# Rows of token operands at 258 words instead of 256, and weight halves at one of eight 8-byte offsets, in a float32 two-model kernel on one core

## The chip, the cores and the metric

The kernel runs on one core of a Trainium2 chip. The metric is the device time of one execution in microseconds; lower is better. A figure of "before" is the median of three runs unless the text names the profiled execution.

## The reference

A sequence of 256 tokens of width 1024 goes through two small models, all in float32. The first is a gated mixer followed by a feed-forward layer:

```python
h = rmsnorm(x, norm_mix_g); proj = h @ w_in
u, v, bg, cg, xs, ga, gb = split(proj)
a = gelu(u) * (chunk-masked mix of rmsnorm(gelu(v)) over 128 tokens)
c = bg * causal_dwconv(cg * xs)
x = x + (sigmoid(ga) * (a @ w_proj_a) + sigmoid(gb) * (c @ w_proj_b)) @ w_out
z = relu(rmsnorm(x) @ w_ff1); x = x + (z * z) @ w_ff2
```

The second has two layers. The first layer's mixer is differential attention with 8 heads, the second's is latent attention with 16 heads; each is followed by a convolutional feed-forward layer (up to 5632 columns, three-tap causal convolution, silu gate, down to 1024). A final RMS norm gives the output. Nearly all the arithmetic is in the products of 256 tokens with weight matrices.

## The kernel before, in words

Activations are kept transposed: a tile `[128, 8, 256]` holds 1024 features as 8 rows `k` of 128 features, each row 256 tokens long. These tiles come from `b8` (line 110), a ring of seven buffers. Smaller ones with four rows come from `b4` (line 113, five buffers), pairs of rows from `t2` (line 116, ten buffers).

For accuracy every float32 product is made of three fast matmuls. An operand `w` is split into `hi`, its rounded half, and `lo`, the remainder, and `mm3` (line 195) adds `hi*xh`, `hi*xl` and `lo*xh` into one PSUM bank; every matmul of these products is issued from line 193. The moving operand is normally a row of tokens (256 columns) and the stationary one a 128x128 block of a weight half. In `token_group` (line 395) and `last_rows` (line 937) the roles are swapped: 128 tokens are stationary and 512 columns of a weight half move.

Weights stream from HBM in pieces of 1024 columns (512 KB). `run` (line 142) goes through a list of steps in program order; ahead of each it loads raw pieces (line 165, on SP's queue, up to five ahead) and splits units (`split_to`, line 168): ScalarE writes `hi` (line 178), VectorE subtracts to get `lo` (line 179). Both halves have a ring of seven buffers, and splitting runs three units ahead of use, so a `hi` buffer comes free when TensorE has finished with the unit that held it.

`group` (line 207) computes four column blocks for eight rows `k`: one row with four column blocks is 12 matmuls, and one unit serves two rows. `rows` (line 222) takes one unit per row and makes all eight column blocks of it, 24 matmuls. So in a `group` the row changes every 12 matmuls and the unit every 24; in `rows` both change every 24.

A row of a `b8` tile begins 1024 bytes after the one before it, a row of a `b4` tile too; a buffer of a weight half is 4096 bytes, and a 128-column block begins 512 bytes after the one before it. Seen modulo 512 bytes, then, the start of the moving row and the start of the weight block stand in one fixed relation all through the kernel, whichever buffers, rows and blocks are at work.

The tiles named `v` (lines 430, 703, 1000) and the final `xt` (line 926) use buffers of the same ring as `b8`, in the shapes `[128, 2, 1024]` and `[128, 2048]`.

Of the kernel before, what the change touches and what calls it, by code (L numbers as in the profile page):

```python
# [11 lines left out]
F32R = mybir.dt.float32r  # L12
# [4 lines left out]
P = 128  # L17
T = 256
D = 1024
# [6 lines left out]
DA_SCALE = 64 ** -0.5  # L26
MLA_SCALE = 96 ** -0.5
LAMBDA_INIT = 0.8 - 0.6 * float(np.exp(-0.3 * 0))
WARM = 11
NEG = float(np.finfo(np.float32).min)  # L30

# [53 lines left out]
class Builder:  # L85
# [22 lines left out]
        return self.act.tile(shape, dt, tag=tag, bufs=bufs, name=self.name(tag))  # L108

    def b8(self, dt=F32):  # L110
        return self.t([P, 8, T], "b8", 7, dt)

    def b4(self, shape, dt=F32):
        return self.t([P] + shape, "b4", 5, dt)
# [27 lines left out]
    def run(self):  # L142
        order, seen = [], set()
        for units, _ in self.steps:
            for u in units:
                if id(u) not in seen:
                    seen.add(id(u))
                    order.append(u)
        at = {id(u): i for i, u in enumerate(order)}
        raws, rat = [], {}  # L150
        for u in order:
            if id(u.raw) not in rat:
                rat[id(u.raw)] = len(raws)
                raws.append(u.raw)
        done = {"split": 0, "raw": 0}

        def load_to(i):
            while done["raw"] <= min(i, len(raws) - 1):
                r = raws[done["raw"]]
                r.tile = self.rawp.tile([P, 1024], F32, tag="raw", name=self.name("raw"))  # L160
                n = r.size if done["raw"] else r.size // 2
                for j, o in enumerate(range(0, r.size, n)):
                    for dst, src in self.before.get((done["raw"], j), ()):
                        self.nc.sync.dma_start(out=dst, in_=src)
                    self.nc.sync.dma_start(out=r.tile[:, o:o + n], in_=r.src[:, o:o + n])
                done["raw"] += 1

        def split_to(i):
            while done["split"] <= min(i, len(order) - 1):
                u = order[done["split"]]  # L170
                load_to(rat[id(u.raw)] + self.RAW_AHEAD)
                w = u.raw.tile[:, u.off:u.off + u.size]
                hi = self.unitp.tile([P, 1024], F32R, tag="hi", name=self.name("hi"))
                lo = self.unitp.tile([P, 1024], F32R, tag="lo", name=self.name("lo"))
                n = u.size if done["split"] else u.size // 2
                for o in range(0, u.size, n):
                    sl = slice(o, o + n)
                    self.last_hi = self.nc.scalar.copy(hi[:, sl], w[:, sl])  # L178
                    (u.eng or self.nc.vector).tensor_tensor(  # L179
                        lo[:, sl], w[:, sl], hi[:, sl].bitcast(F32), op=ALU.subtract)  # L180
                u.hi, u.lo = hi[:, :u.size], lo[:, :u.size]
                done["split"] += 1

        load_to(2)
        split_to(1)
        for units, fn in self.steps:
            if units:
                split_to(max(at[id(u)] for u in units) + self.AHEAD)
            fn()
# [158 lines left out]
    def setup(self):  # L348
# [9 lines left out]
        ps = self.at_bank()  # L358
        for _ in range(WARM):
            nc.tensor.matmul(ps[:, 0, 0:P], self.ones, self.ones, start=True, stop=True)  # L360
# [54 lines left out]
    def mixer(self):  # L415
# [7 lines left out]
        bufs = {}  # L423
# [3 lines left out]

        def v_evac(h):
            if h == 0:
                bufs["v"] = self.t([P, 2, D], "b8", 7)  # L430
                bufs["ssv"] = self.t([P, 2, 2], "ssv", 1)
            v = bufs["v"]
            for b in range(2):
                o = v[:, b, h * 512:(h + 1) * 512]
                nc.scalar.activation(o, vb[h][b].rearrange("p a t -> p (a t)"), AF.Gelu,
                                     scale=st["rt"][:, b:b + 1])
                sq = self.t2()
                nc.scalar.activation(sq.rearrange("p a t -> p (a t)"), o, AF.Square,
                                     accum_out=bufs["ssv"][:, h, b:b + 1])
# [13 lines left out]
        def S(pr):  # L453
            def fn():
                with self.tc.issue_after(self.last_hi.ins):
# [4 lines left out]
                         between={0: (N(1),), 2: (N(2),), 4: (N(3), S(0)), 6: (S(1),), 7: (S(2),)})  # L460
        self.token_group(g[1], vb[1], KD, xh, xl,
                         between={0: (S(3),), 2: (one,), 5: (two, lambda: v_evac(0))})
        self.step(lambda: v_evac(1))
        self.step(v_norm)

# [179 lines left out]
    def diff_attention(self):  # L645
# [4 lines left out]
        st, bufs = {}, {}  # L650

        def one():
# [24 lines left out]
            nc.vector.tensor_tensor(nl, e[:, 1:2], e[:, 0:1], op=ALU.subtract)  # L677
            nc.vector.tensor_scalar(nl, nl, -LAMBDA_INIT, None, op0=ALU.add)
            st["nl"] = nl
            gs = self.const.tile([P, 1], F32, name="g_sub")  # L680
            nc.vector.tensor_scalar(gs, self.par("g_sub"), 1.0 - LAMBDA_INIT, None, op0=ALU.mult)
            st["gs"] = gs
# [17 lines left out]

        def v_evac(h):
            if h == 0:
                bufs["v"] = self.t([P, 2, D], "b8", 7)
                bufs["oh"], bufs["ol"] = self.b8(F32R), self.b8(F32R)
            for b in range(2):
                nc.scalar.activation(bufs["v"][:, b, h * 512:(h + 1) * 512],
                                     vb[h][b].rearrange("p a t -> p (a t)"), AF.Copy,
                                     scale=st["rt"][:, b:b + 1])
# [107 lines left out]
        for p in range(4):  # L816
            bt = {}
            if p == 0:
                bt[2] = (two, lambda: v_evac(0))
                bt[6] = (normed,)  # L820
            if p >= 1:
                bt[4] = (L(scores, 2 * p - 2),)
                bt[5] = (L(scores, 2 * p - 1),)
            if p >= 2:
                bt[3] = (L(trans, p - 2),)
                bt[6] = (L(values, p - 2),)
                bt[7] = (L(out_t, p - 2),)
            bk = []
            self.group(wqk[4 * p:4 * p + 4], bk, 4, xh, xl, between=bt)
            self.step(lambda p=p, bk=bk: qk_evac(p, bk))  # L830
        self.token_group(wv[4:], vb[1], KD, xh, xl,
                         between={0: (L(trans, 2),), 2: (L(scores, 6),), 4: (L(scores, 7),)})
        self.step(lambda: v_evac(1))
        wo = self.weights(a["da_w_o"], 2048, 2)
        oh, ol = lambda k: bufs["oh"][:, k, :], lambda k: bufs["ol"][:, k, :]
# [86 lines left out]
    def turn_x(self, b, c):  # L922

        nc = self.nc
        if b == 0 and c == 0:
            self.xt = self.b8().rearrange("p k t -> p (k t)")
            self.g_last = self.b4([D])
            nc.sync.dma_start(out=self.g_last, in_=self.a["g_last"])
            self.last_sq = self.t([P, 2, 2], "lsq", 1)
        ps = self.at_bank().rearrange("p a t -> p (a t)")  # L930
        for i in range(4):
            nc.tensor.transpose(ps[:, i * P:(i + 1) * P],
                                self.x[:, 4 * c + i, b * P:(b + 1) * P], self.ident)
        o = b * D + c * 512
        nc.scalar.copy(self.xt[:, o:o + 512], ps)
# [46 lines left out]
    def mla(self):  # L982
# [7 lines left out]
        st, skv, sq_, bufs = {}, {}, {}, {}  # L990
# [5 lines left out]
        def tables():  # L996
            ml = self.b4([2, 2, T])
            nc.sync.dma_start(out=ml, in_=a["ml_tab"])
            self.ml_c, self.ml_s = ml[:, 0], ml[:, 1]
            bufs["v"] = self.t([P, 2, D], "b8", 7)  # L1000
            bufs["ke"], bufs["ko"] = self.b8(), self.b8()
            bufs["oh"], bufs["ol"] = self.b8(F32R), self.b8(F32R)
            nc.gpsimd.memset(bufs["ke"][96:128, :, :], 0.0)
            nc.gpsimd.memset(bufs["ko"][0:32, :, :], 0.0)
# [78 lines left out]
        def k_evac(h):  # L1083
            for i in range(2):
                sl = slice(4 * h + 2 * i, 4 * h + 2 * i + 2)
                for key, o in (("ke", 0), ("ko", 64)):
                    nc.scalar.copy(bufs[key][o:o + 64, sl, :], kb[h][i][o:o + 64])

        self.step(tables)
        self.group(w_ckv, kvb, 3, xh, xl)  # L1090
        self.step(one)
# [225 lines left out]
```

## Time and profile before

| | before |
|---|---|
| median of three runs (lowest to highest) | 1029.93 us (1027.82 to 1030.82) |
| the profiled execution, its own time | 1023.16 us |
| its span, first to last instruction | 1021.4 us |
| TensorE busy | 997.7 us (98%) |
| VectorE, ScalarE, GpSimd busy | 745.1, 569.7, 175.0 us |
| HBM read over the span | 178.04 MB, 175 GB/s |
| mean granted TensorE clock | 0.994 of full speed |

The profiled execution is 6.8 us shorter than the median of the runs, and 1.8 us of its time lie outside the span. A matmul's busy time counts its whole passage through the array, and consecutive matmuls overlap; a matmul of 256 columns is listed at 280 ns though a new one starts every 113 to 118 ns. The number to look at is therefore the pitch, the time from one start to the next, which the chain of waits gives: a piece of the chain divided by the matmuls in it.

### The profile page before, as it was taken

What the parts mean: (1) busy time and instruction counts of PE and PEld (TensorE: products, weight loads), DVE (VectorE), ACT (ScalarE), POOL (GpSimd) and SP (SyncE); (2) the same over time, 40 slices, a digit from 0 to 9 for tenths busy, and PEclk for the clock granted to TensorE, in tenths of its full rate; (3) what the DMA queues carried; (4) which work ended last, traced back from release to release, by engine and by line L of the source; (5) the groups of instructions that cost most, each with busy time, mean ns of one, the idle gap of its engine ahead of it and who ended that gap; (6) DMA issues with size and microseconds to landing.
All of it is one profiled execution on the core that took longest, in us unless ns stands there. A gap on an engine that the chain in (4) does not pass through costs nothing.

```text
span 1021.4 us, 19659 instructions
## 1 busy us (share of the span) xinstructions
PE 997.7 (98%) x7940; PEld 960.3 (94%) x7940; DVE 745.1 (73%) x1124; ACT 569.7 (56%) x895; POOL 175.0 (17%) x121
## 2 busy tenths in 40 slices
PE   8999999999999999989899999999998999999996
PEld 7999999999999999978799999999987899999995
DVE  5667766567656665778868887777889988887774
ACT  6644454445444444846576665555686667655553
POOL 2101300002311221452102201010422121100001
PEclk9999999999999999999999999999999999999999
DMA  9675555554555555353345465555553435655531
GB/s 334 220 259 170 185 184 185 189 187 159 202 196 190 194 194 195 113 206 129 109 159 187 158 209 181 194 181 160 176 168 127 145 114 195 205 190 185 187 104 41
DMA packets 51067, 180.36 MB, mean 177 GB/s; under 512 B 5664, under 2 KB 6176, under 8 KB 50976
## 3 DMA queue, kind: packets, MB, share of 16 engines
q1 hardware_dynamic: 50688, 178.58, 51.9%
q8 instruction: 62, 1.02, 0.4%
q10 hardware_dynamic: 288, 0.52, 0.1%
q14 instruction: 29, 0.24, 0.1%
HBM read 178.04 MB, written 1.05 MB: 175 GB/s over the span
## 4 chain that ended last, share of the span: by engine, by line
PE 88%; DVE 3%; ACT 3%; issue 2%; POOL 2%; DMA 1%; SPq 0%; POOLq 0%; DVEq 0%; ACTq 0%
PE mm L193 60%; PE at L193 24%; DVE lo L179 1%; ACT hi L178 1%; POOL tiny L308 1%; POOL xg L697 1%; DMA raw<-in_w_in 1%; PE at L1119 1%; DVE t L870 1%; PE at L1142 1%; ACT b L741 0%; ACT t L1129 0%; POOL t L869 0%; PE at L489 0%; PE at L1118 0%
## 5 line engine op out<-in xcount | busy, mean ns | idle before, releaser
L193 PE MATMUL mm<-b,hi 128*128 128x256 f32 x3584 | 638.6, 280 | 1.1 <-DVE b L1031 0.8
L193 PEld LDWEIGHTS mm<-b,hi 128*128 128x128 f32 x3584 | 547.9, 188 | 5.1 <-issue 2.1
L179 DVE TENSOR_TENSOR lo<-raw,hi 128x1024 fp32r<-128x1024 f32 (+2 forms) x336 | 416.6, 1251 | 181.9 <-ACT hi L178 180.9
L178 ACT CAST hi<-raw 128x1024 fp32r<-128x1024 f32 (+2 forms) x337 | 345.4, 1037 | 301.5 <-PE mm L193 230.4
L193 PE MATMUL mm<-b,lo 128*128 128x256 f32 x1792 | 499.9, 279 | 0.0
L193 PEld LDWEIGHTS mm<-b,lo 128*128 128x128 f32 x1792 | 336.7, 188 | 0.7 <-issue 0.7
L193 PE MATMUL at<-b,hi 128*128 128x256 f32 x1088 | 190.9, 278 | 1.0 <-POOL b L337 1.0
L193 PEld LDWEIGHTS at<-b,hi 128*128 128x128 f32 x1088 | 165.0, 188 | 2.2 <-POOL b L337 1.2
L193 PE MATMUL at<-b,lo 128*128 128x256 f32 x544 | 151.0, 278 | 0.0
L193 PEld LDWEIGHTS at<-b,lo 128*128 128x128 f32 x544 | 102.0, 187 | 0.0
L894 POOL TENSOR_TENSOR t<-t,t 128x512 f32<-128x512 f32 x22 | 40.3, 1833 | 289.9 <-DVE t L597 251.4
L597 DVE SCALAR_TENSOR_TENSOR t<-t,par,t 128x254 f32<-128x254 f32 (+1 forms) x176 | 76.0, 485 | 11.6 <-ACT t L595 11.0
L280 POOL TENSOR_TENSOR t<-t,t 128x512 f32<-128x512 f32 x18 | 26.0, 1445 | 197.5 <-ACT t L279 196.9
L193 PE MATMUL at<-hi,b 128*128 128x512 f32 x176 | 56.7, 394 | 0.0
L336 ACT CAST b<-t 128x512 fp32r<-128x512 f32 x50 | 30.9, 621 | 43.1 <-POOL t L894 36.4
L331 DVE TENSOR_TENSOR t<-mm,rbc 128x512 f32<-128x512 f32 x76 | 51.6, 687 | 0.2
L337 POOL TENSOR_TENSOR b<-t,b 128x512 fp32r<-128x512 f32 x16 | 29.7, 1864 | 119.6 <-ACT b L336 119.6
L193 PE MATMUL mm<-hi,b 128*128 128x512 f32 x144 | 48.8, 411 | 1.1 <-ACT hi L178 1.1
L595 ACT ACTIVATE t<-t,par 128x256 f32<-128x256 f32 x88 | 46.0, 591 | 6.4 <-DVE t L331 6.4
L337 DVE TENSOR_TENSOR b<-t,b 128x512 fp32r<-128x512 f32 x34 | 24.2, 718 | 23.0 <-ACT b L336 23.0
L193 PEld LDWEIGHTS at<-hi,b 128*128 128x128 f32 x176 | 32.9, 187 | 7.7
L193 PEld LDWEIGHTS mm<-hi,b 128*128 128x128 f32 x144 | 27.8, 194 | 8.2 <-ACT hi L178 1.9
(181 smaller groups left out, 709.2 us busy)
## 6 DMA issues: line engine op xcount, KB each, us to landing
raw<-in_ffn_up SPq DMA_DIRECT2D x88, 512.0 KB, 4.8
raw<-in_w_ff SPq DMA_DIRECT2D x64, 512.0 KB, 4.5
raw<-in_w_in SPq DMA_DIRECT2D x55, 512.0 KB, 4.8
raw<-in_ffn_down SPq DMA_DIRECT2D x44, 512.0 KB, 4.1
raw<-in_da_qk SPq DMA_DIRECT2D x16, 512.0 KB, 4.8
raw<-in_w_proj_a SPq DMA_DIRECT2D x8, 512.0 KB, 4.1
raw<-in_w_proj_b SPq DMA_DIRECT2D x8, 512.0 KB, 3.7
raw<-in_w_out SPq DMA_DIRECT2D x8, 512.0 KB, 4.9
```

The source lines that it names most:

```text
L178: self.last_hi = self.nc.scalar.copy(hi[:, sl], w[:, sl])
L179: (u.eng or self.nc.vector).tensor_tensor(lo[:, sl], w[:, sl], hi[:, sl].bitcast(F32), op=ALU.subtract)
L193: self.nc.tensor.matmul(out, lhsT, rhs, start=start, stop=stop, skip_group_check=True)
L280: nc.gpsimd.tensor_tensor(self.ss, self.ss, sq, op=ALU.add)
L308: self.nc.gpsimd.tensor_tensor(r, ms, self.mhalf[:, :n], op=ALU.pow)
L331: self.nc.vector.tensor_tensor(o, bank, self.over2(r), op=ALU.mult)
L336: self.nc.scalar.copy(hi, src)
L337: (eng or self.nc.vector).tensor_tensor(lo, src, hi.bitcast(F32), op=ALU.subtract)
L595: nc.scalar.activation(y, z, AF.Identity, scale=w[2], bias=bias)
L597: nc.vector.scalar_tensor_tensor(out=y[:, d:], in0=z[:, :T - d], scalar=w[2 - d], in1=y[:, d:], op0=ALU.mult, op1=ALU.add)
L697: nc.gpsimd.tensor_tensor(xp, xp, self.over2(st["rx"]), op=ALU.mult)
L894: nc.gpsimd.tensor_tensor(y[0], y[0], y[1], op=ALU.mult)
```

## The change

A `b8` tile gets rows of 258 words and its users see a view of the first 256 of each row; a row then begins 1032 bytes after the one before it. The `v` and `xt` tiles are made as large as the new buffer, with `v`'s two rows 1032 words apart and `xt` contiguous. The buffers of both weight halves grow from 1024 to 1040 words, and the unit with number n in the order of splitting lies at word 2n mod 16 of its buffers, so at one of eight offsets of 0 to 56 bytes; `hi` and `lo` of a unit have the same one. No instruction is added or removed and the order is the same. `b4` and `t2` tiles and the residual `x` stay as they were.

```diff
+XPAD = 2
+WPAD = 16
...
     def b8(self, dt=F32):
-        return self.t([P, 8, T], "b8", 7, dt)
+        t = self.t([P, 8, T + XPAD], "b8", 7, dt)
+        return t[:, :, :T]
...
-                hi = self.unitp.tile([P, 1024], F32R, tag="hi", name=self.name("hi"))
-                lo = self.unitp.tile([P, 1024], F32R, tag="lo", name=self.name("lo"))
+                hi = self.unitp.tile([P, 1024 + WPAD], F32R, tag="hi", name=self.name("hi"))
+                lo = self.unitp.tile([P, 1024 + WPAD], F32R, tag="lo", name=self.name("lo"))
+                o = 2 * done["split"] % WPAD
+                hi, lo = hi[:, o:o + 1024], lo[:, o:o + 1024]
...
-                bufs["v"] = self.t([P, 2, D], "b8", 7)
+                bufs["v"] = self.t([P, 2, D + 4 * XPAD], "b8", 7)[:, :, :D]
...
-            self.xt = self.b8().rearrange("p k t -> p (k t)")
+            self.xt = self.t([P, 8 * (T + XPAD)], "b8", 7)[:, :8 * T]
```

The line of `v` is changed in the same way in three places.

## Rows read from the trace of the kernel before

**Rows 1.** The page, part 1: busy time, share and instructions of each engine.

```profile
PE 997.7 (98%) x7940; PEld 960.3 (94%) x7940; DVE 745.1 (73%) x1124; ACT 569.7 (56%) x895; POOL 175.0 (17%) x121
```

**Rows 2.** The page, part 4: the chain that ended last, by line.

```profile
PE mm L193 60%; PE at L193 24%; DVE lo L179 1%; ACT hi L178 1%; POOL tiny L308 1%; POOL xg L697 1%; DMA raw<-in_w_in 1%; PE at L1119 1%; DVE t L870 1%; PE at L1142 1%; ACT b L741 0%; ACT t L1129 0%; POOL t L869 0%; PE at L489 0%; PE at L1118 0%
```

**Rows 3.** Groups by line and form, PE: xcount | busy us, mean ns | idle.

```profile
L193 PE MATMUL mm<-b,hi 128*128 128x256 f32 x3584 | 638.6, 280 | 1.1 <-DVE b L1031 0.8 <-ACT b L706 0.2
L193 PE MATMUL mm<-b,lo 128*128 128x256 f32 x1792 | 499.9, 279 | 0.0
L193 PE MATMUL at<-b,hi 128*128 128x256 f32 x1088 | 190.9, 278 | 1.0 <-POOL b L337 1.0
L193 PE MATMUL at<-b,lo 128*128 128x256 f32 x544 | 151.0, 278 | 0.0
L193 PE MATMUL at<-hi,b 128*128 128x512 f32 x176 | 56.7, 394 | 0.0
L193 PE MATMUL mm<-hi,b 128*128 128x512 f32 x144 | 48.8, 411 | 1.1 <-ACT hi L178 1.1
L193 PE MATMUL at<-lo,b 128*128 128x512 f32 x88 | 34.7, 394 | 0.0
L193 PE MATMUL mm<-lo,b 128*128 128x512 f32 x72 | 29.5, 409 | 0.8 <-DVE lo L179 0.8
```

**Rows 4.** The chain in order of time: start us, us, what xcount.

```profile
101.05 117.31 PE mm L193 x996
...
320.14 10.88 PE mm L193 x96
331.02 10.88 PE at L193 x96
...
850.70 10.89 PE mm L193 x96
861.59 5.59 PE at L193 x24
867.18 11.31 PE mm L193 x96
```

**Rows 5.** Stretches, PE alone: window, length, busy us (matmuls), granted clock, DMA share, GB/s.

```profile
101.00:252.10 151.10, 151.10 (x1285) 1.00 0.54 180
...
265.80:417.90 152.10, 152.10 (x1343) 1.00 0.56 187
430.50:434.40 3.90, 3.90 (x36) 1.00 0.80 200
437.40:450.80 13.40, 13.40 (x121) 1.00 0.53 190
...
524.90:549.70 24.80, 24.80 (x221) 1.00 0.37 123
...
845.20:861.40 16.20, 16.20 (x145) 1.00 0.43 144
```

**Rows 6.** Timeline of PE around a restart: start us, us, what [idle before <-releaser].

```profile
263.48 0.28 PE L193 MATMUL mm<-b,lo 128*128 128x256 f32 x1
...
263.83 0.28 PE L193 MATMUL mm<-b,lo 128*128 128x256 f32 x1
...
265.59 0.38 PE L193 MATMUL at<-b,hi 128*128 128x256 f32 x1 [1.00 <-POOL b L337]
...
266.15 0.28 PE L193 MATMUL at<-b,lo 128*128 128x256 f32 x1
...
266.49 0.28 PE L193 MATMUL at<-b,lo 128*128 128x256 f32 x1
```

**Rows 7.** Groups by line and form, DVE: xcount | busy us, mean ns | idle.

```profile
L179 DVE TENSOR_TENSOR lo<-raw,hi 128x1024 fp32r<-128x1024 f32 x318 | 399.6, 1267 | 178.1 <-ACT hi L178 177.2
L597 DVE SCALAR_TENSOR_TENSOR t<-t,par,t 128x255 f32<-128x255 f32 x88 | 41.5, 493 | 11.3 <-ACT t L595 11.0
L494 DVE SCALAR_TENSOR_TENSOR t<-at,par,b 128x256 f32<-128x256 f32 x8 | 3.5, 480 | 0.3
```

**Rows 8.** Waits: engine, line, waited for: us in total, times, longest us.

```profile
ACT hi L178 <- PE mm L193: 230.4, 147, 6.6
DVE lo L179 <- ACT hi L178: 180.9, 157, 2.7
```

More of the change, by code (lines that the diff above doesn't have):

```diff
@@ L702, in v_evac @@
             if h == 0:
-                bufs["v"] = self.t([P, 2, D], "b8", 7)
+                bufs["v"] = self.t([P, 2, D + 4 * XPAD], "b8", 7)[:, :, :D]
                 bufs["oh"], bufs["ol"] = self.b8(F32R), self.b8(F32R)
@@ L999, in tables @@
             self.ml_c, self.ml_s = ml[:, 0], ml[:, 1]
-            bufs["v"] = self.t([P, 2, D], "b8", 7)
+            bufs["v"] = self.t([P, 2, D + 4 * XPAD], "b8", 7)[:, :, :D]
             bufs["ke"], bufs["ko"] = self.b8(), self.b8()
```

## The prediction, made before the changed kernel was run

> **What bounds the kernel now.** I began with the busy times: TensorE is busy for 98% of the span, the next engine for 73% [rows 1]. The chain that ended last says the same with more force: 84% of it is matmuls of line 193 [rows 2]. So nothing but the time per matmul, or the few gaps, can move the end. The forms of line 193 come next: 3584 + 1792 + 1088 + 544 = 7,008 matmuls with 256 moving columns, and 176 + 144 + 88 + 72 = 480 with 512 [rows 3]. Their listed 280 and 400 ns overlap, so for the cost of one I divide pieces of the chain [rows 4]. In the mixer 996 matmuls take 117.31 us, 117.8 ns each. In the feed-forward layer 96 take 10.88 us, 113.3 ns each, and the next 96, into the other PSUM banks and with rows of `b4` in place of `b8`, again 10.88. Late in the kernel 96 take 10.89, and two pieces later 96 more of the same loop, with the same `xh` and `xl`, take 11.31.
>
> So identical matmuls have **two pitches**, 113.3 and 117.8 ns, 4.5 ns apart. The clock is not the reason: both stretches are granted 1.00, the 2.4 GHz level, at about the same load of transfers (0.54 and 0.56) [rows 5]. The stretches with the short pitch are the last five of those rows. They hold 1343 + 36 + 121 + 221 + 145 = 1,866 matmuls, of which 16 are transposes of 128 columns (four in the fourth of them, twelve in the last, by the steps of the code): about 1,850 short ones. That leaves about 5,160 of the 7,008 with the long pitch, a few dozen first ones after a gap among them. Where the pitch switches is told by the timeline: up to 264 us three matmuls take 0.35 us, then `at` waits 1.00 us for GpSimd's `b`, and from then on three take 0.34 [rows 6]. After that nothing disturbs the short pitch for 1,343 matmuls, whatever VectorE, ScalarE and the transfers do. A gap can throw it either way; between gaps it holds.
>
> **The change part by part.** Nothing is added, removed or reordered; all that changes is where operands lie. Three effects are possible.
>
> *Reads of TensorE.* While one matmul streams its row, the weights of the next are loaded (the weight loads are as busy as the matmuls, 960.3 us [rows 1]). If the two reads get in each other's way at some places of the memory, the pitch depends on the places and on the phase between them. In the old layout the places are always in one relation modulo 512 bytes, so a phase that is established can last, and rows 4 and 6 show phases that last hundreds of matmuls. In the new one a row moves 8 bytes against the one before it and a unit 8 bytes against the unit before: the relation changes every 12 or 24 matmuls, up to 7,008 / 12 = 584 times, where now only a gap between matmuls changes the phase. The trace before holds no matmul with such offsets, so I bound the price. Best by the nearest rows: all 5,160 go to the short pitch, 5,160 x 4.48 ns (11.31 less 10.88 us, over 96) = 23.1 us saved. Worst by those rows: the 1,850 short ones go to the long pitch, 1,850 x 4.48 = 8.3 us lost. Still further out on the good side: 256 columns at 2.4 GHz are 106.7 ns, 6.6 below the shortest pitch, and 512 are 213.3 where 24 take 5.59 us, 233 each [rows 4]; but no stretch comes near either, so I don't count on it. Which value? If a change of relation is a new throw like a gap, the share of short ones stays at 1,850 in 7,008, 26%, and nothing is gained. If the short pitch holds once it is hit, whatever the relation, all end there. I take the middle of these two: half of the 5,160, 2,580 x 4.48 = **11.6 us saved**. The 480 wide ones I leave at their pitch.
>
> *Writes and reads of the vector engines.* The splits now write 8 to 56 bytes off, and operands of two rows have a gap of 8 bytes between them. VectorE's convolution taps already read and write 4 bytes off: 493 ns for 255 elements, against 480 for 256 elements with no such shift [rows 7]. That bounds it at 3%; over the split's 399.6 us it would be 11 us of VectorE's time, none of it on the path as long as the split waits for ScalarE for 180.9 us in all [rows 8]. ScalarE shows no shifted operand. From nothing to the same 3% on its `hi`, about 30 ns of a step that waits 230.4 us for TensorE to give a buffer back [rows 8]: cost nothing. If that cover were gone, in the attention stretches where TensorE waits, it would be 30 ns on some dozens of splits, 1 to 2 us. I take 0, and keep 2 us for the upper end.
>
> *Transfers.* Raw pieces land in tiles that are not moved, and the output leaves from `xt`, which stays contiguous: 0.
>
> **Sum.** 1023.16 - 11.6 = 1011.6 us against the profiled execution. That one is 6.8 us under the median of the runs, 1029.93. Against the median: 1029.93 - 11.6 = **1018.3**, and since it is medians that are compared, I give 1018. A measurement of this kernel can tell about 0.3%, 3 us, from no change.
>
> **The rivals.**
>
> *A. The pitch has nothing to do with places.* For it: the 996 matmuls at one pitch run through 83 rows and some 40 units, so through the seven buffers several times [rows 4], and the switch at 265 us came from a wait alone [rows 6]. All the same, every one of those places has the same remainder modulo 512, so these rows don't exclude a dependence on the last bits. The time would be 1029.9, within 3 us up or down for gaps that fall otherwise. The Trainium skill speaks for this one, and against the change: its page "SBUF — State Buffer", section "Who interferes with whom", says that TensorE and ScalarE never wait on anyone, and "TensorE: Matmul & The Clock Gate", "Step-by-step: what each phase is for", gives TensorE two independent read ports, one for the moving operand, one for weights. By that the sum would be 1029.9. The trace agrees that other engines don't disturb the pitch; it doesn't say what makes the two pitches.
>
> *B. The short pitch is what the aligned relation allows, and the change takes it away (slower).* Place: the long feed-forward stretch, 1,343 matmuls without a break [rows 5]. If the first row that starts 8 bytes off throws TensorE out of the short rhythm and no gap follows, the stretch runs at 117.8, and so do the other four: 8.3 us, 1029.9 + 8.3 = 1038.2. It decides as soon as fewer than 26% of the matmuls are short afterwards. For it: a read that starts off its natural boundary may need one piece more. Against: the long pitch is already the state of three quarters of the matmuls, so there is little left to lose.
>
> *C. The long pitch can't last under moving offsets.* All matmuls are short: 1029.9 - 23.1 = 1006.8. For it: a rhythm that closes in itself is what a fixed relation would make, and the change removes just that. Against: a moving relation could as well break the short one.
>
> *D. The views don't move anything*, for instance because a row's pad is lost in a reshape. The shapes in the diff say otherwise; the time would be A's.
>
> **How the numbers follow.** My forecast, some of the matmuls gained, has 0.32; C has 0.16; A with D 0.25; B 0.27, in it a pitch above the long one, which no row prices. Faster by over 0.3% is forecast and C: 0.48. Within 0.3%: 0.25. Slower: 0.27. The range reaches from a little below C, 1005, to B with the 2 us of the splits, rounded down to 1039; beyond it lie the cheaper wide matmuls on one side and a dearer misaligned read on the other, 1 in 10 each. The forecast's own range is 1007 to 1027.
>
> **What would show it.** In the chain of the changed kernel, 96 matmuls of a `group` should take 10.88 to 11.3 us and differ from group to group, or all take 10.88 (C). If pieces take 11.31 in the same stretches as before, it is A. If the pieces between 266 and 418 us take 11.3, it is B, and above 11.4 a dearer read. Pitches within a group that change every 12 matmuls would show that the places matter. The subtraction of line 179 should keep its 1.27 us. I am wrong if the pitch is as before in every stretch, or if the wide matmuls carry the difference.

## The result, and the profile after

The changed kernel takes 1036.82 us (median of three, 1036.41 to 1037.45) against 1029.93: 1.0072 times as long, 95% interval 1.0046 to 1.0097. It is slower by 6.9 us, where 1018 had been forecast. Its profiled execution takes 1036.82 us with a span of 1035.0, so that execution is at its median, while the one of before lay 6.8 us under its own; for that reason the two traces differ by 13.6 us of span and not by 6.9.

The page's part 1 and part 4 of the changed kernel (lines have moved by five):

```profile
PE 1012.6 (98%) x7940; PEld 975.9 (94%) x7940; DVE 744.7 (72%) x1124; ACT 569.4 (55%) x895; POOL 173.1 (17%) x121
...
PE mm L198 60%; PE at L198 25%; DMA raw<-in_w_in 1%; ACT hi L183 1%; PE at L1124 1%; POOL xg L702 1%; POOL tiny L313 1%; PE at L1147 1%; DVE t L875 1%; ACT b L746 0%; POOL t L285 0%; ACT t L1134 0%; POOL t L874 0%; PE at L1123 0%; PE at L494 0%
```

The second line is shown to be read beside [rows 2]: the bound is the same, TensorE with line 198, and the other engines' busy times have not grown. Against [rows 1] TensorE's own is 14.9 us longer. So the matmuls themselves cost more. The chain in order of time (start us, us, what) tells where:

```profile
101.47 118.65 PE mm L198 x996
...
313.17 11.40 PE at L198 x96
324.57 11.47 PE mm L198 x96
336.04 11.50 PE at L198 x96
...
863.00 11.45 PE mm L198 x96
874.45 5.58 PE at L198 x24
880.03 11.42 PE mm L198 x96
```

Against [rows 4], the 996 matmuls of the mixer go from 117.8 to 119.1 ns each (118.65 / 996). In the feed-forward layer 96 matmuls, 10.88 us before, take 11.40 to 11.50. Late in the kernel both pieces take 11.42 to 11.45; the one that had the short pitch has lost it. The 24 wide matmuls are as before. Neither of the two steady pitches is left.

The granted clock is no part of it. The stretches (window, length, busy us and matmuls, clock, DMA share, GB/s):

```profile
101.40:255.00 153.60, 153.60 (x1294) 1.00 0.54 179
267.80:427.00 159.20, 159.20 (x1342) 1.00 0.53 179
```

1,342 matmuls take 159.2 us where 1,343 took 152.1 [rows 5], at 1.00, the 2.4 GHz level, in both.

Within a `group` the pitch now alternates from row to row. Here is the timeline of TensorE in the mixer, of which only those lines are shown at which a new row begins; between two of them lie 12 matmuls:

```profile
151.29 0.40 PE L198 MATMUL mm<-b,hi 128*128 128x256 f32 x2
...
152.71 0.40 PE L198 MATMUL mm<-b,hi 128*128 128x256 f32 x2
...
154.17 0.40 PE L198 MATMUL mm<-b,hi 128*128 128x256 f32 x2
...
155.59 0.41 PE L198 MATMUL mm<-b,hi 128*128 128x256 f32 x2
...
157.04 0.40 PE L198 MATMUL mm<-b,hi 128*128 128x256 f32 x2
...
158.45 0.40 PE L198 MATMUL mm<-b,hi 128*128 128x256 f32 x2
...
159.89 0.40 PE L198 MATMUL mm<-b,hi 128*128 128x256 f32 x2
```

Rows 0 to 5 take 1.42, 1.46, 1.42, 1.45, 1.41 and 1.44 us. An odd row begins 8 bytes past a multiple of 16, an even one on a multiple. Taken over the whole trace (the time from one start of line 198 to the next, gaps of 130 ns or more left out), the mean is 118.0 ns on the even rows of `b8` and 120.2 ns on the odd ones, some 2,600 matmuls each. Grouped by the weights' start, at 0 or 8 past a multiple of 16, the means are 118.84 and 118.95 ns: the weights' own start makes no difference that can be seen. Grouped by both, an even row takes 118.1 ns with weights at 0 and 118.0 with weights at 8, an odd one 120.3 and 120.0 (1,220 to 1,382 matmuls each). The distance between row and weights is a multiple of 16 for the even rows with weights at 0 and for the odd rows with weights at 8, and not for the other two; so the price goes with the row's own start and not with that distance. The same mean in the trace of before is 116.6 ns over all.

The vector engines pay nothing. Groups by line and form on VectorE (xcount | busy us, mean ns | idle), and two waits:

```profile
L184 DVE TENSOR_TENSOR lo<-raw,hi 128x1024 fp32r<-128x1024 f32 x318 | 398.8, 1264 | 190.9 <-ACT hi L183 190.4 <-PE mm L198 0.5
...
L602 DVE SCALAR_TENSOR_TENSOR t<-t,par,t 128x255 f32<-128x255 f32 x88 | 41.5, 493 | 11.1 <-ACT t L600 10.6
```

```profile
ACT hi L183 <- PE mm L198: 240.8, 148, 4.5
DVE lo L184 <- ACT hi L183: 195.1, 164, 2.7
```

The subtraction that writes at the offsets takes 1264 ns, 1267 before [rows 7], and the splits wait a little longer for TensorE than in [rows 8].

### The profile page after: what moved, and what is told of

The parts are those of the page before. It is cut to its first block, busy times and chain, and to the rows that moved or that the text cites. A ratio compares the mean times of both kernels' runs of the same rounds, so it can differ in the third digit from the quotient of the medians.

```text
span 1035.0 us, 19659 instructions
## 1 busy us (share of the span) xinstructions
PE 1012.6 (98%) x7940; PEld 975.9 (94%) x7940; DVE 744.7 (72%) x1124; ACT 569.4 (55%) x895; POOL 173.1 (17%) x121
## 4 chain that ended last, share of the span: by engine, by line
PE 89%; POOL 3%; ACT 2%; DVE 2%; issue 2%; DMA 1%; SPq 0%; POOLq 0%; DVEq 0%; ACTq 0%
PE mm L198 60%; PE at L198 25%; DMA raw<-in_w_in 1%; ACT hi L183 1%; PE at L1124 1%; POOL xg L702 1%; POOL tiny L313 1%; PE at L1147 1%; DVE t L875 1%; ACT b L746 0%; POOL t L285 0%; ACT t L1134 0%; POOL t L874 0%; PE at L1123 0%; PE at L494 0%
## 5 line engine op out<-in xcount | busy, mean ns | idle before, releaser
L198 PE MATMUL mm<-b,hi 128*128 128x256 f32 x3584 | 649.6, 283 | 0.7 <-DVE b L1036 0.4
L198 PE MATMUL mm<-b,lo 128*128 128x256 f32 x1792 | 505.1, 282 | 0.0
L198 PE MATMUL at<-b,hi 128*128 128x256 f32 x1088 | 195.2, 282 | 0.9 <-POOL b L342 0.9
L602 DVE SCALAR_TENSOR_TENSOR t<-t,par,t 128x254 f32<-128x254 f32 (+1 forms) x176 | 76.0, 485 | 11.4 <-ACT t L600 10.6
L198 PE MATMUL at<-lo,b 128*128 128x512 f32 x88 | 34.8, 395 | 0.0
```

Source lines behind the costliest of these rows:

```text
L198: self.nc.tensor.matmul(out, lhsT, rhs, start=start, stop=stop, skip_group_check=True)
L602: nc.vector.scalar_tensor_tensor(out=y[:, d:], in0=z[:, :T - d], scalar=w[2 - d], in1=y[:, d:], op0=ALU.mult, op1=ALU.add)
```

## The experiments

The theory drawn from this trace had two parts. **S**: a moving row that starts 8 bytes past a multiple of 16 costs about 2 ns by itself. **P**: the two steady pitches belong to the fixed relation of the operands, and go with it. The rivals: what counts is only that the relation keeps moving (R); or the pitch is thrown by gaps and the places have no part (G).

**First four: one part of the change at a time.** The rows alone:

```diff
-                o = 2 * done["split"] % WPAD
+                o = 0
```

> Rows of 258 words as in the change, all weight halves at offset 0. Theory S (the start of a moving row counts: one that begins 8 bytes past a multiple of 16 costs about 2.1 ns more per matmul, the weights' start costs nothing): the odd rows of b8 tiles, some 2,600 matmuls, run near 120 ns, the even ones near 118; with the short pitch broken too this is as slow as the full change, 6 to 8 us over before. Theory R (what counts is that the relation of row and weight block keeps moving, not where a row starts): odd and even rows alike, and half of the change's loss or more, 3 to 7 us.

The weights' offsets alone, rows 256 words apart:

```diff
-XPAD = 2
+XPAD = 0
```

> Rows of 256 words as before, weight halves at one of eight offsets. Theory S: no matmul above 118 ns for its place; at worst the short stretches are lost, so between 0 and 8 us over before, and no odd-even pattern. Theory R: the relation moves with each unit, every 24 matmuls, so the pitches scatter between 113 and 123 ns as in the changed kernel, 3 to 7 us over before.

Rows moving by 16 bytes instead of 8, weights at offset 0:

```diff
-XPAD = 2
+XPAD = 4
...
-                o = 2 * done["split"] % WPAD
+                o = 0
```

> Rows of 260 words, so every row starts at a multiple of 16 bytes, but the rows still move against the weights, by 16 bytes each; weight halves at offset 0. Theory S: no row costs more for its start, the mean pitch stays within 113 to 118 ns, the time within 3 us of before. Theory R: the same scatter as in the changed kernel and 3 to 7 us over before.

Rows as before, all weights at the offset of 8 bytes:

```diff
-XPAD = 2
+XPAD = 0
...
-                o = 2 * done["split"] % WPAD
+                o = 2
```

> Rows of 256 words, every weight half at the one offset of 8 bytes, so the relation is fixed again but 8 bytes other than before. Theory S: two steady pitches of 113.3 and 117.8 ns as before, time within 8 us of before either way by where the gaps fall. Theory R in its form that a certain relation excludes the short pitch or allows nothing else: all matmuls at one pitch, 8 us over or 23 us under before.

Measured, against 1030.31 us of the kernel before on the same chips (25 runs, 1023.36 to 1033.36); the pitch is the mean worked out as above:

| kernel | median us | ratio to before, interval | pitch, `b8` rows |
|---|---|---|---|
| rows alone | 1036.23 | 1.0067 (1.0042 to 1.0092) | even 118.2, odd 119.9 ns |
| weights alone | 1032.40 | 1.0036 (1.0015 to 1.0058) | 118.3 ns |
| rows by 16 bytes | 1031.32 | 1.0022 (1.0004 to 1.0041) | 118.0 ns |
| weights at 8 bytes | 1032.89 | 1.0039 (1.0022 to 1.0057) | 118.3 ns |

Pieces of the chain of each, in this order: the one from the same place in the mixer, and for the last three also one of the feed-forward layer:

```profile
101.82 118.67 PE mm L198 x996
```

```profile
100.93 117.74 PE mm L198 x996
...
288.91 11.20 PE at L198 x96
```

```profile
101.04 117.51 PE mm L198 x996
...
356.48 11.28 PE at L198 x96
```

```profile
101.88 117.73 PE mm L198 x996
...
301.27 11.41 PE mm L198 x96
```

The rows alone reproduce the change, 118.67 us against 118.65, and it is their 8 bytes that do it: moving by 16 bytes costs 1.16 us less over the 996 and 4.9 us less over the kernel. Some 2,600 odd-row matmuls at 1.7 ns more are 4.4 us. That bears S out. All four have lost the steady short pitch, also the three with no row off a multiple of 16: in the stretch between 277 and 400 us their pieces of 96 take 11.2 to 11.4 us where before had 10.88. So far R was not excluded.

The fourth kernel was meant to hold the relation fixed, and didn't. The buffers of the weight halves are 1040 words in all four, so from one buffer to the one beside it the place moves by 64 bytes modulo 512; its sequence of pitches repeats every seven units, the number of buffers. Theory S had expected two steady pitches there and was wrong with that layout. That turned out useful: the places of all operands are known from the order of allocation, and these traces hold many distances between the moving row and the block being loaded. Grouped by distance modulo 512, stretches in which the row stood 192 bytes past the `hi` block and 320 past the `lo` block ran at 113.3 ns for all but their first matmuls; where both distances were 0 modulo 128, most ran at 120.0. The kernel before has 64 and 64 everywhere.

**Next three: the distance fixed, and chosen.** All are the kernel before with buffers and rows of their old sizes, with an unused gap ahead of the ring of `lo` (`gap_a`), behind it (`gap_b`), or both. No instruction differs. The first has both:

```diff
         self.unitp = ent(tc.tile_pool(name="unit", bufs=self.UNIT_BUFS))
+        ent(tc.tile_pool(name="gap_a", bufs=1)).tile([P, 96], F32, name="gap_a")
+        self.lop = ent(tc.tile_pool(name="unit_lo", bufs=self.UNIT_BUFS))
+        ent(tc.tile_pool(name="gap_b", bufs=1)).tile([P, 64], F32, name="gap_b")
...
-                lo = self.unitp.tile([P, 1024], F32R, tag="lo", name=self.name("lo"))
+                lo = self.lop.tile([P, 1024], F32R, tag="lo", name=self.name("lo"))
```

> Rows of 256 words and buffers of 1024 as before; unused gaps ahead of the buffers of the lo halves and behind them put the moving row 192 bytes past the hi block and 320 past the lo block, modulo 512 (before: 64 and 64). Theory P (the pitch is set by the fixed distance of the two operands modulo 512, and the four runs before had 113.3 ns wherever this pair of distances stood by chance): all 256-column matmuls at 113.3 ns, about 5,100 of them 4.5 ns shorter, 20 to 25 us under before. Theory G (pitch is thrown by gaps alone, any fixed distance behaves like the old one): both pitches again, within 8 us of before.

With a `gap_a` of 32 words and no `gap_b`:

> The same with 192 for hi and 64 for lo, which equals the pair of the kernel beside it modulo 256 only. Theory P with period 256: the same 20 to 25 us under before. Theory P with period 512: some other pitch between 115 and 120 ns, within 15 us of before. Theory G: both old pitches, within 8 us of before.

With no `gap_a` and a `gap_b` of 112 words:

> The same with distances 0 and 0. Theory P: in the four runs before, stretches in which both operands stood at distance 0 modulo 128 ran at 120 ns; so all 256-column matmuls near 120.0 ns, 3.4 ns more on 7,008 matmuls than the mean of before (116.6), 20 to 28 us over before. Theory G: both old pitches, within 8 us of before.

Against 1029.31 us of before beside them (1028.45 to 1030.32): 1004.34 us for 192 and 320, ratio 0.9763 (0.9746 to 0.9781); 1002.78 us for 192 and 64, 0.9743 (0.9728 to 0.9759); 1043.32 us for 0 and 0, 1.0139 (1.0121 to 1.0157). The chain of the first, 192 and 320:

```profile
98.45 112.93 PE mm L196 x996
...
311.77 10.88 PE mm L196 x96
```

of the second, 192 and 64:

```profile
98.50 112.93 PE mm L195 x996
...
311.82 10.88 PE mm L195 x96
322.70 10.88 PE at L195 x96
...
834.36 10.92 PE mm L195 x96
845.28 5.53 PE at L195 x24
850.80 10.93 PE mm L195 x96
```

and of the third, 0 and 0:

```profile
102.34 119.51 PE mm L195 x996
...
292.98 11.52 PE at L195 x96
304.50 11.52 PE mm L195 x96
```

Every piece of 256-column matmuls shown is at 113.3 to 113.9 ns in the first two (10.88 / 96, 10.93 / 96) and at 120.0 in the third (119.51 / 996, 11.52 / 96). The same instructions in the same order lie around them. G is out, and R with it: the distance stands still in all three. The pair 192 and 64 equals 192 and 320 modulo 256 only and does the same, so places 256 bytes apart are alike here. The price of 0 and 0 came out lower than expected, 14 us and not 20 to 28: its 3.4 ns over 7,008 matmuls are 23.8 us against the trace of before, which is itself 6.8 us under its median; wide matmuls at 228 ns for 233 give back 2.4 more.

**Last three: the price of a row's start in a fixed relation.** On top of 192 and 64, all `b8` tiles begin 2 words, or as a control 4 words, later in a larger buffer (8448 bytes, so all rows keep one distance modulo 256; the `v` and `xt` tiles get buffers of that size too):

```diff
     def b8(self, dt=F32):
-        return self.t([P, 8, T], "b8", 7, dt)
+        t = self.t([P, 8 * T + 64], "b8", 7, dt)[:, 2:2 + 8 * T]
+        return t.rearrange("p (k t) -> p k t", t=T)
```

> The layout with hi at 192 and lo at 64, but every b8 row starts 8 bytes later, so at 8 past a multiple of 16, always; distances 200 and 72, fixed; b4 rows as before. Theory S (a row that starts off a multiple of 16 costs about 2 ns by itself): the 5,250 matmuls with b8 rows cost 1.7 to 2.2 ns more than those of the kernel beside it with 16 in place of 8, so 9 to 12 us between the two. Theory D (only the distance counts): between the two at most 3 us, or a difference of either sign that comes with another steady pitch.

> The control: every b8 row 16 bytes later, distances 208 and 80, all at multiples of 16. Theory S: no price for the start, so 9 to 12 us under the kernel with 8 bytes; its own pitch is between 113.3 (if the good place is broad) and 118 ns, 1003 to 1028 us. Theory D: equal to the one with 8 bytes within 3 us.

The third leaves the rows where they were and has a `gap_b` of 32 words and no `gap_a`:

> Distances 192 for both halves. If each load has its own price by its own distance (theory P1), hi at 192 keeps 113.3 ns and only the loads of lo, a third, can be longer: 113.3 to 115.6 ns on the mean, 1002 to 1019 us. If the rhythm needs the 128 bytes between hi and lo (theory P2), there are one or two longer pitches, 116 to 120 ns, 1022 to 1043 us.

Against 1029.48 us of before beside them (1024.19 to 1031.01): 1043.36 us with the rows at 8 (1.0141, 1.0111 to 1.0171), 1031.03 us at 16 (1.0022, 0.9993 to 1.0052). Two pieces of each chain; first rows at 8, then rows at 16:

```profile
316.91 10.92 PE at L196 x96
327.82 11.69 PE mm L196 x96
```

```profile
312.18 10.95 PE at L196 x96
323.12 11.42 PE mm L196 x96
```

In both kernels the second part of the feed-forward layer, `at`, moves rows of `b4`, which stayed where they were: 113.8 and 114.1 ns. The first part moves rows of `b8`: 121.8 ns at 8 bytes, 119.0 at 16. The 2.8 ns between them, times some 5,250 matmuls, are 14.7 us, and 12.3 us were measured. That is what S expected in a fixed relation, at a price somewhat above its 1.7 to 2.2 ns. Theory D is not ruled out by this pair: the distances of the two differ as well, and each runs at one steady pitch, 11.69 or 11.42 us for 96, which D allowed for. What speaks against D is the changed kernel's own trace, where an odd row costs 2.0 to 2.2 ns more whether its distance to the weights is a multiple of 16 or not; how much of the 2.8 ns here is the start's and how much the distance's stays open. The control also shows how narrow the good place is: 16 bytes further, 5 ns are lost.

The kernel with 192 and 192 took 1015.80 us, within P1's bounds. Its four runs lie at 1008.6, 1015.5, 1016.1 and 1027.0 us; the ratio, 0.9852 (0.9805 to 0.9899), is that of the first three, and the fourth lies within P2's bounds. Its trace does not show what P1 said:

```profile
98.70 112.89 PE mm L195 x996
...
314.23 11.31 PE mm L195 x96
325.54 11.31 PE at L195 x96
...
847.39 10.90 PE mm L195 x96
```

It has the two pitches of before, 113.3 in the mixer and 117.8 in the feed-forward layer, only in other stretches than [rows 4]. So with equal distances of 64 modulo 128 a stretch can settle at either pitch, and only the kernels with 128 bytes between `hi` and `lo` show the short one alone: P2's condition, mostly with a better time than P2's bounds. That other pairs 128 bytes apart would do the same is not shown.

## Why the prediction was wrong

**What bounds the kernel** was read rightly: nothing but the time per matmul moved, and the transfers and vector engines cost nothing, as the prediction had it (11 us of VectorE's time in the worst case; none in the trace). Its 3% for a shifted operand was no real bound, since the two rows compared also differ in what they read (`t` in one, `at`, a PSUM bank, in the other).

**The step that failed** is the one called "Which value?". It weighed only how often the short pitch would be hit again, "half of the 5,160", on the ground that the short pitch might hold "whatever the relation". It doesn't. Under moving places no pitch lasts beyond a unit of 24 matmuls; single matmuls scatter (5th to 95th percentile 114 to 123 ns on the even rows) about a mean of 118.0 ns, 0.2 above the old long pitch. Instead of 11.6 us won, nothing is won from the 5,160, which lose 1.0 us, and the 1,850 short ones lose 4.7 ns each, 8.7 us.

**The term that was missing** is the start of the row. Rival B named a read that starts off its natural boundary as a reason, but the sum had no term for it. Some 2,600 odd-row matmuls at 2.1 ns more than the even ones are 5.5 us. Together that makes 15.2 us against the profiled execution, where the span grew by 13.6; TensorE's idle time shrank by 1.3 us (1021.4 less 997.7 against 1035.0 less 1012.6). Against the median it is 6.9. The runs of before range from 1023.36 to 1033.36 us; that most of them hold fewer short stretches than the profiled one would account for the difference, but only one execution of it has a trace, so this is argued and not shown. For it speaks the kernel with rows moving by 16 bytes: it has lost the short pitch too, and its median is only 1.0 us over that of before. Of the 5.9 us that the rows alone cost in the median, then, 4.9 go with their 8 bytes, so against the median the missing term weighs more than the lost short pitch.

**Rival B** had the sign, the place and nearly the time (1038.2 against 1036.82): the long feed-forward stretch went from 113.3 to about 119 ns, its pieces of 96 lying at 11.16 to 11.52 us about the 11.4 that was to mark a dearer read. Its chance had been put at 0.27. That its time came so near is in part luck: its 8.3 us are the profiled execution's short matmuls set on the median, with nothing for the row's start. **Rival C** failed as forecast, for the moving places made no stretch short; its ground, that a fixed relation is what makes the long pitch, was half right: the relation decides, but the cure is another fixed one, not a moving one; the 1006.8 us it priced are reached, and passed, by the kernel with 192 and 64. **Rival A** fell. The two sections of the Trainium skill that the prediction cited for it, in "SBUF — State Buffer" ("Who interferes with whom") and "TensorE: Matmul & The Clock Gate" ("Step-by-step: what each phase is for"), have TensorE's two reads independent and never waiting; with nothing changed but unused gaps beside the ring of `lo`, the time went from 1002.78 to 1043.32 us. The measurement decides: the places of the two operands set the pitch. That other engines don't disturb it remains true of these traces. For the price of a row's start, the Trainium skill's page "SBUF — State Buffer", section "Specifications (TRN2)", has a line that the prediction did not use: SBUF has lines of 16 bytes, and each crossing to a new one costs. The odd rows of the changed kernel agree with it, at 2.0 to 2.2 ns a matmul; that one more line is the reason is not shown by any run.

## What to carry to other kernels

When identical instructions run at two steady rates, divide pieces of the chain by their counts and ask what was fixed, before varying it: here the cure was a better constant distance between the moving rows and the weight blocks (one unused gap of 128 bytes, 26.5 us, 2.6%), and moving the operands about cost 0.7%. Keep the rows that TensorE streams on multiples of 16 bytes: 8 bytes off cost about 2 ns of some 118 here. And if a pad is to shift one thing, look at what else its buffer's size shifts: from buffer to buffer the places moved by 64 bytes modulo 512, which was in no one's plan.

## What the runs showed that was not expected

The pitch of a 256-column float32 matmul goes with the distance between the row being streamed and the block being loaded. With 192 and 64 (or 320) bytes to `hi` and `lo` it is 113.3 ns; with 64 and 64, or 192 and 192, either 113.3 or 117.8; with 208 and 80, 119.0; with 0 and 0, 120.0; with 200 and 72, rows off a multiple of 16, 121.8. What in the memory makes it so stays open. It isn't shown either that the distance alone counts: by the order of allocation, wherever 192 and 64 (or 320) lasted at 113.3 ns, row, `hi` and `lo` also began at the same three places modulo 256. Only 0 and 0 was met at two places, 64 bytes apart, and took 120.0 ns at both. The best place for the wide matmuls, whose weights move and whose tokens stand still, is open too: 24 of them took 5.53 us at 192 and 64 and 5.58 in the changed kernel, and no run was made for them alone. That 113.3 ns is the least that any place allows is not shown either; it is the least seen.
